# Encoder trunk on one core: mLSTM value products in full fp32 from unsplit weights, and another order of fills and first head

## The chip, the cores and the metric

The kernel runs on one core of one Trainium2 chip. The metric is the device time of one execution in microseconds; the time before is the median of three runs. The profile comes from one execution of its own, whose time stands beside its span below. PE is TensorE, DVE VectorE, ACT ScalarE, POOL GpSimd; SP's queue issues most loads.

## The reference

A trunk of two layers on 512 positions of width 1024 (batch 1, fp32). Layer 0 mixes by pooling and attention, layer 1 by a bidirectional matrix memory (mLSTM), and each layer ends with a SwiGLU mixer. The change is in layer 1's mixer, which is, in short:

```python
def mlstm_mixer(h, w_in, conv_w, conv_b, gate_b, head_gain, w_out):
    z = h @ w_in                                    # q,k | v | o | gates
    qk = silu(centred_depthwise_conv(qk_raw, conv_w, conv_b))
    ...
    h_fwd = mlstm_chunkwise(q, k, v, g[0, 0], log_sigmoid(g[0, 1]))
    h_bwd = flip(mlstm_chunkwise(flip(q), flip(k), flip(v), ...))
    hs = rms_norm((h_fwd + h_bwd)...) * head_gain
    return (sigmoid(o) * hs).reshape(B, S, -1) @ w_out
# per head and direction, with b = cumsum(log f):
#   D[t, s] = b[t] - b[s] + i[s]  (s <= t),   m[t] = max over s
#   s[t, s] = (q[t] . k[s]) * exp(D[t, s] - m[t])
#   h[t]    = sum_s s[t, s] v[s] / max(|sum_s s[t, s]|, exp(-m[t]))
```

There are 8 heads; a head has 64 query and key columns and 128 value columns. The chunked scan of the reference computes the same as this sum over all s.

## The kernel before

**Number forms.** Products of activations and weights are made of three fp32r matmuls, high x high, high x low and low x high part (`mm3`, through `mm` at line 79). A slab of weights is 256 columns of a matrix: two loads of 512 KB on SP's queue, and for each an ACT cast to the high part (`whi`) and a DVE subtraction to the low part (`wlo`), in `split` (lines 117 and 121). At most three slabs are loaded or in use; `free_slabs` starts the next.

**Layer 1's mixer** is `odd`. It begins with a gate stage (some 580 to 640 us): the projection of pair 0's queries and keys and of its values together with the gates; then `gate_chain`, a generator that computes the running sums and maxima of the gates in steps, and beside it, one step of the chain for each step of these, the projections `project_qk` and `project_v` of pair 1. Pair p holds heads 2p and 2p+1. `take_qk` takes a projection through the 5-tap convolution and the SiLU: per half (queries, keys) an ACT copy into `pad`, ACT and four DVE taps into `cy` (lines 1050 to 1054), tanh, a product, and conversions into fp32r high and low parts (`unit`, lines 1063 to 1071). `pad` and `cy` have one buffer each, in a pool `gc` of the gate stage.

Then `memory` computes the heads, in 10 slots. The pool `pw` that holds its tiles is opened when the pools of the gate stage are closed, in their place; a tile waits for the ones that were there. Slot h holds `weights(h)`: for each direction three matmuls that put the exponents into two banks (`pbd`, `pbm`) and seven exponentials (lines 1177 and 1181) that write `w`, 1280 columns: the 10 of 16 blocks of 128 x 128 that the direction needs; four `scores(h, sb)`: two matmuls and three or four DVE products that multiply `w` (lines 1194 and 1199); `halves(h)`: `w` is split into an fp32r high part `ph` (ACT, line 117) and low part `pl` (DVE, line 121). The value products of a head, `values(h, tb)`, are made in the next slot, and `finish(h)`, which normalises a head, gates it and turns it into the output projection's input, in the slot after that. In the last slots the output projection `project` begins.

Between these, `fill(n)` takes n steps of a generator of work that no head waits for at once, of 32 steps per piece: three products of 256 columns to a step, or, for queries and keys, three of 512 columns to two steps. The pieces of before: output gate 0, pair 2's queries and keys, output gate 1, values 2, queries and keys 3, output gate 2, values 3, output gate 3. `FILL = (16, 2, 2)`: 16 steps behind `weights`, 2 behind each `values`, 2 behind each `scores`.

**Banks.** Of the eight, three go around among `pbd`, `pbm`, `psS` (scores), the gates' banks and `phT`, five among all the rest: projections, value products (`ppv`), output projection.

**Order.** A scheduler sorts each engine's instructions: what was written first goes first if a simulated time line has it ready, and later work may go ahead of what is not. Engines then run their instructions in that order. `behind(ins)` forbids that an engine's instructions written inside it go ahead of `ins` on that engine.

Of the kernel before, what the change touches and what calls it, by code (L numbers as in the profile page):

```python
# [15 lines left out]
P = 128  # L16
# [18 lines left out]
WINDOW_STEPS = (1, 3, 8, 13)  # L35
POOL_STEP = 12
FILL = (16, 2, 2)
LOW_HALVES = "vv"
GATE_STEPS = (10, 10)


# [14 lines left out]
class Trunk:  # L56
# [835 lines left out]
    def odd(self, x):  # L892
        nc, a, tc = self.nc, self.a, self.tc
        with ExitStack() as es:
# [13 lines left out]
            with ExitStack() as es2:  # L908
                gp = self.open(es2, "gp", 1, side="right")
                zg = gp.tile([P, NTB, 32], F32, name="zg")  # L910
                tri = gp.tile([P, 2, P], F32, name="tri")
                nc.scalar.dma_start(tri, a["k_mask"].rearrange("d p t -> p d t"))
                nc.gpsimd.tensor_copy(self.tri, tri)
                s0 = self.next_slab()
                gw = self.gate_weights(gp)
                self.want(*[(a["w_od"][i], e) for i, e in (
                    (qk[1], "v"), (vs[1], "v"), (og[0], "v"), (qk[2], "v"), (og[1], "v"), (vs[2], "v"), (qk[3], "v"),
                    (og[2], "v"), (vs[3], "v"), (og[3], "v"))])
                self.load_slabs()
                v0 = self.values_tile()  # L920
                qk0 = [self.bank(f"pqk{1 + i % 2}") for i in range(4)]
                for hf in range(2):
                    ts = slice(hf * HS, (hf + 1) * HS)
                    pv = [self.bank("pvg") for _ in range(2)]
                    gens = [self.gemm_nat(pv[j][:, 0:288], gw, x, 2 * hf + j, 0, 288) for j in range(2)]
                    g2 = [self.gemm(qk0[2 * hf + b][:, 0:HS], s0, b, x, ts) for b in range(2)]
                    if hf == 0:
                        gens, g2 = g2 + gens, []
                    for k in range(KD):
                        for gg in gens:  # L930
# [17 lines left out]
                box = []  # L948
                for _ in self.project_qk(gc, 1, x, box):
                    next(gates, None)  # L950
                st[1] = box.pop()
                for _ in self.project_v(1, x, box):
                    next(gates, None)
                vals = {0: v0, 1: box.pop()}
                drain(gates)
            pw_es = es.enter_context(ExitStack())
            pw = self.open(pw_es, "pw", 1, side="right")
# [5 lines left out]
            self.memory(pw, x, st, vals, proj)  # L963
            pw_es.close()
            self.xp = self.open(self.ctx, "xq", 1)
            self.restore()
# [38 lines left out]

    def values_tile(self):

        t = self.od.tile([P, NTB, 2, 258], F32R, name="vx", tag="vx", bufs=2)
        self.nc.vector.tensor_copy(t[:, :, :, 256:258], self.ones[:, 0:16].rearrange("p (a b c) -> p a b c", a=4, b=2))
        return t  # L1010

    def take_values(self, vx, tb, ps):
        pv = ps.rearrange("p (h d) -> p h d", h=2)
        self.split(vx[:, tb, :, 0:128], vx[:, tb, :, 128:256], pv)

    def project_v(self, p, x, box):
        vx = self.values_tile()
# [5 lines left out]
        self.free_slabs()  # L1023
        box.append(vx)

    def project_qk(self, pool, p, x, box):
        slab = self.next_slab()
        pss = []
        for b in range(2):
            ps = self.bank("pqk")  # L1030
            for _ in self.gemm(ps, slab, b, x, slice(0, S)):
                yield
                yield
            pss.append([ps])
        self.free_slabs()
        box.append(self.take_qk(pool, p, pss))

    def take_qk(self, pool, p, pss):

# [96 lines left out]
        self.free_slabs()  # L1136
        box.append(og)

    def memory(self, pw, x, st, vals, tail):

        nc = self.nc
        off = ({0: 512, 1: 896, 2: 1152}, {3: 512, 2: 896, 1: 1152})
        span = tuple({sb: ((sb + 1, NTB) if d == 0 else (0, sb)) for sb in off[d]} for d in range(2))
        og, wt, parts, sums = {}, {}, {}, {}

        def due():
            box = []
            for kind, p in (("o", 0), ("q", 2), ("o", 1), ("v", 2), ("q", 3), ("o", 2), ("v", 3), ("o", 3)):
                if kind == "o":
                    yield from self.project_o(p, x, box)  # L1150
                    og[p] = box.pop()
                elif kind == "q":
                    yield from self.project_qk(pw, p, x, box)
                    st[p] = box.pop()
                else:
                    yield from self.project_v(p, x, box)
                    vals[p] = box.pop()

        rest = due()

        def fill(n, g=rest):
            for _ in range(n):
                next(g, None)

        def weights(h):
            for d in range(2):
                w = pw.tile([P, 1280], F32, name="w", tag="w", bufs=2)
                r = d * 32 + h
                row = self.idp[:, r:r + 1].broadcast_to([P, P])
                bd, bc = self.bank("pbd"), self.bank("pbm")  # L1170
                nc.tensor.matmul(bd, lhsT=row, rhs=self.nm, start=True, stop=False)
                nc.tensor.matmul(bd.rearrange("p (b t) -> p b t", t=P), lhsT=self.idp,
                                 rhs=self.tri[:, d:d + 1, :].broadcast_to([P, NTB, P]), start=False, stop=True)
                nc.tensor.matmul(bc, lhsT=row, rhs=self.nm, start=True, stop=True)
                for sb in range(NTB):
                    c = slice(sb * P, (sb + 1) * P)
                    nc.scalar.activation(w[:, c], bd[:, c], AF.Exp, bias=self.u_nat[:, d, sb, h:h + 1], scale=1.0)
# [7 lines left out]
        def scores(h, sb):  # L1185
# [2 lines left out]
            ps = self.bank("psS")  # L1188
            c = slice(sb * P, (sb + 1) * P)
            nc.tensor.matmul(ps, lhsT=kd[:, c], rhs=qd, start=True, stop=False)  # L1190
            nc.tensor.matmul(ps, lhsT=kd[:, c], rhs=ql, start=False, stop=True)
            for d in range(2):
                w = wt[h, d]
                nc.vector.scalar_tensor_tensor(w[:, c], ps[:, c], 0.03125, w[:, c], op0=ALU.mult, op1=ALU.mult)
# [4 lines left out]
                    nc.vector.scalar_tensor_tensor(w[:, o:o + n], ps[:, t0 * P:t1 * P], 0.03125, w[:, o:o + n],  # L1199
                                                   op0=ALU.mult, op1=ALU.mult)  # L1200

        def halves(h):
            for d in range(2):
                ph = pw.tile([P, 1280], F32R, name="ph", tag="ph", bufs=2)
                pl = pw.tile([P, 1280], F32R, name="pl", tag="pl", bufs=2)
                self.split(ph, pl, wt.pop((h, d)), lo_eng=LOW_HALVES[d])
                parts[h, d] = (ph, pl)

        def where(d, sb, tb):
            if sb == tb:  # L1210
                return slice(sb * P, (sb + 1) * P)
# [2 lines left out]

        def values(h, tb, between):
            vx = vals[h // 2]
            po = []
            for d in range(2):
                ps = self.bank("ppv")[:, 0:258]
                sbs = range(tb + 1) if d == 0 else range(tb, NTB)  # L1220
                seq = [(sb, i) for sb in sbs for i in range(2)]
                for n, (sb, i) in enumerate(seq):
                    nc.tensor.matmul(ps, lhsT=parts[h, d][i][:, where(d, sb, tb)], rhs=vx[:, sb, h % 2], start=(n == 0),  # L1223
                                     stop=(n == len(seq) - 1))
                po.append(ps)
            if tb == 0:
                sums[h] = pw.tile([P, NTB, P], F32, name="hs", tag="hs", bufs=2)
            both = self.sm.tile([P, HS], F32, name="hb", tag="hm")
            nd = pw.tile([P, 2], F32, name="nd", tag="nd", bufs=4)
            for d in range(2):  # L1230
                nc.scalar.activation(nd[:, d:d + 1], po[d][:, 256:257], AF.Abs)
            next(between, None)
            nc.vector.tensor_tensor(nd, nd, self.floor[:, :, tb, h], op=ALU.max)
            nc.vector.reciprocal(nd, nd)
            next(between, None)
            nc.scalar.activation(both, po[0][:, 0:256], AF.Identity, scale=nd[:, 0:1])
            nc.vector.scalar_tensor_tensor(both, po[1][:, 0:256], nd[:, 1:2], both, op0=ALU.mult, op1=ALU.add)
            next(between, None)
            nc.vector.tensor_tensor(sums[h][:, tb], both[:, 0:128], both[:, 128:256], op=ALU.add)
            next(between, None)  # L1240

        def finish(h):
# [22 lines left out]
        for slot in range(10):  # L1265
            old = finish(slot - 2) if slot >= 2 else iter(())
            if slot < 8:
                weights(slot)
            if slot < 8:
                fill(FILL[0])  # L1270
            else:
                drain(rest)
                fill(16 if slot == 8 else 4, tail)
# [9 lines left out]
                    scores(slot, sb)  # L1283
                    fill(FILL[2])
            drain(old)
            if slot < 8:
                halves(slot)


def constants():  # L1290
# [101 lines left out]
```

## Time and profile before

| | |
|---|---|
| median of three runs | 1237.44 us (1235.94 to 1244.37) |
| profiled execution | 1235.73 us, span 1233.9 us |
| PE | 1208.7 us busy, 98% |
| DVE | 682.2 us, 55% |
| ACT | 500.8 us, 41% |
| POOL | 136.6 us, 11% |
| granted PE clock, mean | 0.994 |

Busy times are shares of the span. Matmuls are pipelined and drawn longer than the time from one to the next, so the PE's share is no measure of its pace. In the rows, L79 is the helper through which all projections go; their banks tell them apart: `pqk` queries and keys, `pv` values, `po` output gates, `pout` output projection. A full fp32 matmul stands as two rows of the PE, an fp32r one as one; the rows' types say f32 for both.

### The profile page before, as it was taken

How to read it: one execution, taken by the hardware profiler on the slowest of the kernel's cores; microseconds unless marked ns; L12 is line 12 of the kernel's file. 1: busy time of each engine (PE TensorE's matmuls, PEld its weight loads, DVE VectorE, ACT ScalarE, POOL GpSimd, SP SyncE). 2: the span in 40 equal slices, each digit the busy share in tenths (PEclk: the TensorE clock that was granted, in tenths of full speed). 3: DMA queues.
4: the chain of work that ended last, by engine and by line, in shares of the span. 5: the costliest groups of instructions: out<-in, count | busy, mean ns of one | idle time of the engine just before them, and what ended most of it. 6: DMA issues, size and time to landing. Idle time of an engine off the chain costs nothing.

```text
span 1233.9 us, 17427 instructions
## 1 busy us (share of the span) xinstructions
PE 1208.7 (98%) x6930; PEld 1030.8 (84%) x6930; DVE 682.2 (55%) x1174; ACT 500.8 (41%) x950; POOL 136.6 (11%) x151
## 2 busy tenths in 40 slices
PE   8999999999999999999998998999999999999998
PEld 6675789988888888889896987989988888888888
DVE  4575866465755476336787887766632323233223
ACT  4466764432122221224567776743532223221321
POOL 0033220111001100110000101110011001100110
PEclk9999999999999999999999998999999999999999
DMA  9515612256745375233431211232242323233232
GB/s 389 222 57 206 234 35 93 95 223 237 275 160 215 137 278 199 76 96 127 148 103 35 68 36 35 69 99 87 90 137 86 120 69 119 86 103 103 70 101 78
DMA packets 43170, 160.19 MB, mean 130 GB/s; under 512 B 4560, under 2 KB 11344, under 8 KB 36944
## 3 DMA queue, kind: packets, MB, share of 16 engines
q1 hardware_dynamic: 42240, 158.75, 37.0%
q8 instruction: 54, 0.88, 0.3%
q10 hardware_dynamic: 848, 0.33, 0.1%
q14 instruction: 28, 0.23, 0.1%
HBM read 154.87 MB, written 4.19 MB: 129 GB/s over the span
## 4 chain that ended last, share of the span: by engine, by line
PE 91%; DVE 4%; ACT 2%; DMA 1%; issue 1%; POOL 0%; SPq 0%; DVEq 0%; ACTq 0%; POOLq 0%
PE pf L79 53%; PE pout L79 12%; PE po L79 3%; PE pv L79 3%; PE z L79 3%; PE ppv L1223 3%; PE pqk L79 2%; PE pu L79 2%; PE pav L875 2%; PE pada L79 1%; PE ppt L863 1%; DVE wlo L121 1%; PE psc L841 1%; PE pvg L79 1%; PE psc L842 1%
## 5 line engine op out<-in xcount | busy, mean ns | idle before, releaser
L79 PE MATMUL pf<-p_lo,whi 128*128 128x512 f32 (+1 forms) x1024 | 383.0, 376 | 0.0
L79 PE MATMUL pf<-p_hi,wlo 128*128 128x512 f32 (+1 forms) x1024 | 382.7, 376 | 0.0
L79 PE MATMUL pf<-p_hi,whi 128*128 128x512 f32 (+1 forms) x1024 | 380.4, 377 | 1.2 <-ACT p_hi L366 1.2
L117 ACT CAST whi<-wraw 128x1024 fp32r<-128x1024 f32 (+1 forms) x193 | 190.8, 1025 | 333.0 <-PE pf L79 238.2
L121 DVE TENSOR_TENSOR wlo<-wraw,whi 128x1024 fp32r<-128x1024 f32 (+1 forms) x193 | 230.3, 1223 | 127.8 <-ACT whi L117 125.5
L79 PEld LDWEIGHTS pf<-p_hi,wlo 128*128 128x128 f32 x1024 | 192.5, 188 | 35.1
L79 PEld LDWEIGHTS pf<-p_lo,whi 128*128 128x128 f32 x1024 | 192.7, 188 | 34.8
L79 PEld LDWEIGHTS pf<-p_hi,whi 128*128 128x128 f32 x1024 | 190.9, 188 | 35.8 <-ACT p_hi L366 1.4
L121 POOL TENSOR_TENSOR p_lo<-gf,p_hi 128x512 fp32r<-128x512 f32 (+1 forms) x48 | 70.5, 1472 | 582.5 <-ACT p_hi L117 582.5
L675 DVE TENSOR_TENSOR gf<-pf,si 128x512 f32<-128x512 f32 (+1 forms) x48 | 31.1, 647 | 164.3 <-PE pf L79 149.4
L79 PE MATMUL pout<-p_hi,whi 128*128 128x256 f32 x320 | 91.5, 287 | 0.3 <-DVE xT L333 0.3
L79 PE MATMUL pout<-p_lo,whi 128*128 128x256 f32 x320 | 90.7, 284 | 0.0
L79 PE MATMUL pout<-p_hi,wlo 128*128 128x256 f32 x320 | 90.0, 283 | 0.0
L117 ACT CAST p_hi<-gf 128x512 fp32r<-128x512 f32 (+1 forms) x48 | 27.9, 582 | 114.7 <-DVE gf L675 114.7
L246 DVE SCALAR_TENSOR_TENSOR aacc<-araw,silc,aacc 128x1024 f32<-128x1024 f32 x49 | 65.4, 1335 | 13.2 <-DMA araw<-in_ada_r_dram 11.8
L79 PEld LDWEIGHTS pout<-p_hi,whi 128*128 128x128 f32 x320 | 61.1, 191 | 3.0 <-issue 1.5
L79 PEld LDWEIGHTS pout<-p_lo,whi 128*128 128x128 f32 x320 | 61.2, 191 | 0.4
L79 PEld LDWEIGHTS pout<-p_hi,wlo 128*128 128x128 f32 x320 | 60.9, 191 | 0.4
L718 DVE SCALAR_TENSOR_TENSOR xT<-pf,mod,xT 128x512 f32<-128x512 f32 x32 | 24.0, 749 | 67.1 <-PE pf L79 66.9
L673 ACT ACTIVATE si<-pf 128x512 f32<-128x512 f32 (+1 forms) x48 | 26.7, 557 | 75.7 <-PE pf L79 75.6
L79 PE MATMUL pout<-unit,whi 128*128 128x256 f32 x256 | 47.6, 285 | 0.8 <-ACT unit L1261 0.8
L333 DVE SCALAR_TENSOR_TENSOR xT<-pout,mod,xT 128x256 f32<-128x256 f32 x64 | 28.9, 479 | 30.7 <-PE pout L79 30.5
(253 smaller groups left out, 1875.2 us busy)
## 6 DMA issues: line engine op xcount, KB each, us to landing
wraw<-in_w_dram SPq DMA_DIRECT2D x130, 512.0 KB, 4.6
araw<-in_ada_r_dram SPq DMA_DIRECT2D x40, 1024.0 KB, 6.4
wraw<-in_w_od_dram SPq DMA_DIRECT2D x24, 512.0 KB, 4.6
araw<-in_ada_a_dram SPq DMA_DIRECT2D x8, 1024.0 KB, 15.7
wraw<-in_w_eo_dram SPq DMA_DIRECT2D x10, 512.0 KB, 4.7
wraw<-in_w_oo_dram SPq DMA_DIRECT2D x10, 512.0 KB, 3.7
wraw<-in_w_qkv_dram SPq DMA_DIRECT2D x6, 512.0 KB, 15.2
wraw<-in_w_dram SPq DMA_DIRECT2D x10, 256.0 KB, 2.7
```

What stands on the lines that cost most here:

```text
L79: self.pe_last = self.nc.tensor.matmul(*args, **k)
L117: nc.scalar.copy(hi, src)
L121: eng.tensor_tensor(lo, src, hi.bitcast(F32), op=ALU.subtract)
L246: nc.vector.scalar_tensor_tensor(acc, src, s, acc, op0=ALU.mult, op1=ALU.add)
L333: nc.vector.scalar_tensor_tensor(xs, ps, self.mcol(layer, vec, m), xs, op0=ALU.mult, op1=ALU.add)
L673: nc.scalar.activation(si[:, :n], p1, AF.Silu)
L675: ins = nc.vector.tensor_tensor(gf[:, :n], p3, si[:, :n], op=ALU.mult)
L718: nc.vector.scalar_tensor_tensor(self.xT[:, m], ps, self.mcol(layer, 5, m), self.xT[:, m], op0=ALU.mult, op1=ALU.add)
L841: nc.tensor.matmul(ps, lhsT=self.qst[:, h, qs], rhs=self.kst[:, 2 * kv], start=True, stop=False)
L842: self.sc_ins = nc.tensor.matmul(ps, lhsT=self.qst[:, h, qs], rhs=self.kst[:, 2 * kv + 1], start=False, stop=True)
L875: nc.tensor.matmul(po[c, 0:HS], lhsT=self.vst[:, k, c], rhs=pt_of[pr, j][:, k], start=(k == 0), stop=(k == 3), tile_position=(0, 64 * j))
L1223: nc.tensor.matmul(ps, lhsT=parts[h, d][i][:, where(d, sb, tb)], rhs=vx[:, sb, h % 2], start=(n == 0), stop=(n == len(seq) - 1))
```

## The change

Five things change:

1. The value products use `w` itself, in fp32, and values in fp32: `halves` goes, the values' low part goes, and a value tile has 130 columns for a head (128 values and two ones) in place of 258. The two directions' sums go into one bank, and the division and sum of the two directions take 128 columns in place of 256, with one addition less.
2. `w` gets four buffers in place of two.
3. The fills become one list, `due`, that begins with values 1 and queries and keys 1; 62 of its steps are taken beside the gate chain and the rest in `memory`. So pair 1's values come ahead of its queries and keys (their slabs too), and the last step of the latter and their `take_qk` fall into slot 0, with `pad` and `cy` in `pw`.
4. A `fill` in `memory` is put behind the second last matmul of the list `core` (the last exponent matmul of each direction, and the second matmul of each score).
5. In slot 0 the scores come right behind the weights, with two steps behind each, and the other 24 steps behind them.

```diff
+                vals, self.og = {0: v0}, {}
+                rest = self.due(x, st, vals)
+                for _ in range(62):
+                    next(rest)
                     next(gates, None)
-                st[1] = box.pop()
-                for _ in self.project_v(1, x, box):
-                    next(gates, None)
-                vals = {0: v0, 1: box.pop()}
                 drain(gates)
...
-        t = self.od.tile([P, NTB, 2, 258], F32R, name="vx", tag="vx", bufs=2)
-        self.nc.vector.tensor_copy(t[:, :, :, 256:258], self.ones[:, 0:16].rearrange("p (a b c) -> p a b c", a=4, b=2))
+        t = self.od.tile([P, NTB, 2, 130], F32, name="vx", tag="vx", bufs=2)
+        self.nc.vector.memset(t[:, :, :, 128:130], 1.0)
...
-        pv = ps.rearrange("p (h d) -> p h d", h=2)
-        self.split(vx[:, tb, :, 0:128], vx[:, tb, :, 128:256], pv)
+        self.nc.scalar.copy(vx[:, tb, :, 0:128], ps.rearrange("p (h d) -> p h d", h=2))
...
-        box.append(self.take_qk(pool, p, pss))
+        box.append(self.take_qk(self.pw, p, pss))
...
+    def due(self, x, st, vals):
+
+        box = []
+        for kind, p in (("v", 1), ("q", 1), ("o", 0), ("q", 2), ("o", 1), ("v", 2), ("q", 3), ("o", 2), ("v", 3), ("o", 3)):
...
+        core = [None, None]
 
         def fill(n, g=rest):
-            for _ in range(n):
-                next(g, None)
+            with self.behind(core[-2]):
+                for _ in range(n):
+                    next(g, None)
...
-                w = pw.tile([P, 1280], F32, name="w", tag="w", bufs=2)
+                w = pw.tile([P, 1280], F32, name="w", tag="w", bufs=4)
...
-                nc.tensor.matmul(bc, lhsT=row, rhs=self.nm, start=True, stop=True)
+                core.append(nc.tensor.matmul(bc, lhsT=row, rhs=self.nm, start=True, stop=True))
...
-            nc.tensor.matmul(ps, lhsT=kd[:, c], rhs=ql, start=False, stop=True)
+            core.append(nc.tensor.matmul(ps, lhsT=kd[:, c], rhs=ql, start=False, stop=True))
...
-        def halves(h):
-            for d in range(2):
-                ph = pw.tile([P, 1280], F32R, name="ph", tag="ph", bufs=2)
-                pl = pw.tile([P, 1280], F32R, name="pl", tag="pl", bufs=2)
-                self.split(ph, pl, wt.pop((h, d)), lo_eng=LOW_HALVES[d])
-                parts[h, d] = (ph, pl)
...
-            for d in range(2):
-                ps = self.bank("ppv")[:, 0:258]
-                sbs = range(tb + 1) if d == 0 else range(tb, NTB)
-                seq = [(sb, i) for sb in sbs for i in range(2)]
-                for n, (sb, i) in enumerate(seq):
-                    nc.tensor.matmul(ps, lhsT=parts[h, d][i][:, where(d, sb, tb)], rhs=vx[:, sb, h % 2], start=(n == 0),
-                                     stop=(n == len(seq) - 1))
-                po.append(ps)
+            ps = self.bank("ppv")[:, 0:260].rearrange("p (d c) -> p d c", d=2)
+            seq = [(d, sb) for d in range(2) for sb in (range(tb + 1) if d == 0 else range(tb, NTB))]
+            for n, (d, sb) in enumerate(seq):
+                nc.tensor.matmul(ps[:, d], lhsT=wt[h, d][:, where(d, sb, tb)], rhs=vx[:, sb, h % 2], start=(n == 0),
+                                 stop=(n == len(seq) - 1))
...
-            for d in range(2):
-                nc.scalar.activation(nd[:, d:d + 1], po[d][:, 256:257], AF.Abs)
+            nc.scalar.activation(nd.rearrange("p (d c) -> p d c", d=2), ps[:, :, 128:129], AF.Abs)
...
-            nc.scalar.activation(both, po[0][:, 0:256], AF.Identity, scale=nd[:, 0:1])
-            nc.vector.scalar_tensor_tensor(both, po[1][:, 0:256], nd[:, 1:2], both, op0=ALU.mult, op1=ALU.add)
+            nc.scalar.activation(both[:, 0:P], ps[:, 0, 0:P], AF.Identity, scale=nd[:, 0:1])
+            nc.vector.scalar_tensor_tensor(sums[h][:, tb], ps[:, 1, 0:P], nd[:, 1:2], both[:, 0:P], op0=ALU.mult, op1=ALU.add)
...
-            nc.vector.tensor_tensor(sums[h][:, tb], both[:, 0:128], both[:, 128:256], op=ALU.add)
...
+            if slot == 0:
+                for sb in range(NTB):
+                    scores(0, sb)
+                    fill(FILL[2])
+                fill(FILL[0] + 4 * FILL[1])
+                continue
...
-            if slot < 8:
-                halves(slot)
```

## Rows read from the trace of the kernel before

**Rows 1.** Windows (us from the start): length, each engine's busy time (instructions), clock, DMA.

```profile
640.00:700.00 60.00, 55.11 (x352) 47.43 (x351) 49.74 (x118) 44.45 (x117) 5.76 (x9) 0.97 0.16 54
...
730.00:760.00 30.00, 24.26 (x148) 21.80 (x148) 24.43 (x57) 21.25 (x56) 2.74 (x4) 0.89 0.12 36
760.00:820.00 60.00, 60.00 (x473) 58.30 (x473) 44.98 (x124) 38.55 (x113) 7.27 (x12) 1.00 0.17 54
820.00:840.00 20.00, 18.21 (x137) 16.49 (x136) 11.93 (x32) 8.36 (x26) 1.21 (x2) 1.00 0.41 132
```

**Rows 2.** Groups by form, PE, 640 to 840 us: busy us, mean ns, idle before.

```profile
L1223 PE MATMUL ppv<-vx,ph 128*128 128x258 f32 x160 | 41.3, 291 | 2.9 <-ACT pad L1050 0.8 <-ACT ph L117 0.8 <-ACT hb L1236 0.7
...
L79 PE MATMUL po<-whi,p_hi 128*128 128x256 f32 x125 | 36.7, 294 | 4.2 <-ACT hb L1236 2.0 <-DVE hb L1237 1.7 <-ACT og L1134 0.5
...
L79 PE MATMUL pout<-unit,whi 128*128 128x256 f32 x123 | 23.3, 288 | 0.8 <-ACT unit L1261 0.8
L79 PE MATMUL pv<-wlo,p_hi 128*128 128x256 f32 x64 | 18.1, 282 | 0.0
...
L1190 PE MATMUL psS<-unit 128*128 128x512 f32 x32 | 13.8, 430 | 1.4 <-ACT w L1181 0.6 <-DVE w L1194 0.5 <-ACT w L1177 0.3
...
L79 PE MATMUL pqk<-p_lo,whi 128*128 128x512 f32 x32 | 12.6, 393 | 0.0
...
L1174 PE MATMUL pbm<-nm,ident 128*128 128x512 f32 x15 | 6.4, 423 | 2.5 <-ACT w L1177 2.5
```

**Rows 3.** Chain that ended last, dense runs: start us, us, what and how many.

```profile
63.21 0.79 PE prs L79 x8
...
721.34 4.79 PE pqk L79 x21
...
765.42 1.43 PE po L79 x12
...
799.09 1.20 PE ppv L1223 x10
...
852.18 0.44 PE pbc L79 x4
```

**Rows 4.** The same chain at the first head.

```profile
638.82 0.23 PE pbd L1172
639.06 11.52 PE po L79 x96
...
655.60 0.62 ACT unit L1070
...
656.24 1.14 ACT w L1177 x4
657.38 1.10 ACT w L1181 x3
```

**Rows 5.** Waits of the PE, 735 to 752 us: total us, times, longest.

```profile
PE po L79 <- ACT hb L1236: 2.0, 1, 2.0
PE po L79 <- DVE hb L1237: 1.7, 1, 1.7
PE pbm L1174 <- ACT w L1177: 1.1, 1, 1.1
```

**Rows 6.** The same chain behind that stretch, and at the last head.

```profile
750.93 5.49 PE po L79 x24
...
831.70 0.70 ACT unit L1261
...
832.42 0.76 DVE unit L1262
```

**Rows 7.** Groups by form, DVE and then ACT, 600 to 840 us.

```profile
L1054 DVE SCALAR_TENSOR_TENSOR cy<-pad,cols,cy 128x512 f32<-128x512 f32 x32 | 24.0, 751 | 2.9 <-ACT cy L1051 2.5
L121 DVE TENSOR_TENSOR pl<-w,ph 128x1280 fp32r<-128x1280 f32 x16 | 23.6, 1485 | 0.3 <-ACT ph L117 0.3
...
L117 ACT CAST ph<-w 128x1280 fp32r<-128x1280 f32 x16 | 19.8, 1263 | 2.6 <-DVE w L1194 2.5
```

More of the change, by code (lines that the diff above doesn't have):

```diff
@@ L37 @@
 FILL = (16, 2, 2)
-LOW_HALVES = "vv"
 GATE_STEPS = (10, 10)
@@ L916, in odd @@
                 self.want(*[(a["w_od"][i], e) for i, e in (
-                    (qk[1], "v"), (vs[1], "v"), (og[0], "v"), (qk[2], "v"), (og[1], "v"), (vs[2], "v"), (qk[3], "v"),
+                    (vs[1], "v"), (qk[1], "v"), (og[0], "v"), (qk[2], "v"), (og[1], "v"), (vs[2], "v"), (qk[3], "v"),
                     (og[2], "v"), (vs[3], "v"), (og[3], "v"))])
@@ L947, in odd @@
                 next(gates)
-                box = []
-                for _ in self.project_qk(gc, 1, x, box):
+                vals, self.og = {0: v0}, {}
+                rest = self.due(x, st, vals)
+                for _ in range(62):
+                    next(rest)
                     next(gates, None)
-                st[1] = box.pop()
-                for _ in self.project_v(1, x, box):
-                    next(gates, None)
-                vals = {0: v0, 1: box.pop()}
                 drain(gates)
             pw_es = es.enter_context(ExitStack())
-            pw = self.open(pw_es, "pw", 1, side="right")
+            self.pw = self.open(pw_es, "pw", 1, side="right")
             self.mix = ([None] * KD, [None] * KD)
@@ L962, in odd @@
             proj = self.project(0, slabs, range(4), self.mix, KD, 1, 2, acc[0])
-            self.memory(pw, x, st, vals, proj)
+            self.memory(st, vals, rest, proj)
             pw_es.close()
@@ L1024, in project_v, with project_qk @@
         box.append(vx)
-    def project_qk(self, pool, p, x, box):
+    def project_qk(self, p, x, box):
         slab = self.next_slab()
@@ L1137, in project_o, with memory @@
         box.append(og)
-    def memory(self, pw, x, st, vals, tail):
-        nc = self.nc
+    def due(self, x, st, vals):
+        box = []
+        for kind, p in (("v", 1), ("q", 1), ("o", 0), ("q", 2), ("o", 1), ("v", 2), ("q", 3), ("o", 2), ("v", 3), ("o", 3)):
+            if kind == "o":
+                yield from self.project_o(p, x, box)
+                self.og[p] = box.pop()
+            elif kind == "q":
+                yield from self.project_qk(p, x, box)
+                st[p] = box.pop()
+            else:
+                yield from self.project_v(p, x, box)
+                vals[p] = box.pop()
+    def memory(self, st, vals, rest, tail):
+        nc, pw, og = self.nc, self.pw, self.og
         off = ({0: 512, 1: 896, 2: 1152}, {3: 512, 2: 896, 1: 1152})
         span = tuple({sb: ((sb + 1, NTB) if d == 0 else (0, sb)) for sb in off[d]} for d in range(2))
[L1144 to L1159, printed above, removed]
+        wt, sums = {}, {}
+        core = [None, None]
         def fill(n, g=rest):
-            for _ in range(n):
-                next(g, None)
+            with self.behind(core[-2]):
+                for _ in range(n):
+                    next(g, None)
         def weights(h):
             for d in range(2):
-                w = pw.tile([P, 1280], F32, name="w", tag="w", bufs=2)
+                w = pw.tile([P, 1280], F32, name="w", tag="w", bufs=4)
                 r = d * 32 + h
@@ L1216, in values @@
             vx = vals[h // 2]
-            po = []
-            for d in range(2):
-                ps = self.bank("ppv")[:, 0:258]
-                sbs = range(tb + 1) if d == 0 else range(tb, NTB)
-                seq = [(sb, i) for sb in sbs for i in range(2)]
-                for n, (sb, i) in enumerate(seq):
-                    nc.tensor.matmul(ps, lhsT=parts[h, d][i][:, where(d, sb, tb)], rhs=vx[:, sb, h % 2], start=(n == 0),
-                                     stop=(n == len(seq) - 1))
-                po.append(ps)
+            ps = self.bank("ppv")[:, 0:260].rearrange("p (d c) -> p d c", d=2)
[3 more added lines that the diff above has]
+                                 stop=(n == len(seq) - 1))
             if tb == 0:
```

## Prediction

> **What bounds the kernel now.** The windows view comes first, to find where TensorE (PE) is not the limit [rows 1]. Between 760 and 820 us it is busy for all 60 us at full granted clock; in 640 to 700 us 4.9 us are idle and the granted clock falls to 0.97 of full speed on the mean, in 730 to 760 us 5.7 and 0.89, and after 820 us 1.8 are idle. All three lie in the mLSTM's memory stage, 640 to 840 us. A busy PE is not a PE at its pace (a matmul that stands alone is drawn 0.3 to 0.5 us long), so I count instead. The forms of the PE in that stage [rows 2]: 320 value products (two rows of 160), 377 for the output gate (three rows), 192 for later values (three), 181 of the output projection (two), 64 scores (two), 96 of the query and key projection (three), 43 for the weights' exponents (three), and 32 transposes of 128 columns, near the 0.110 us of the 128-wide products. What one costs in a dense run is read from the chain that ended last [rows 3]: 4.79/21 = 0.228 us at 512 columns, 1.43/12 = 0.119 at 256, 1.20/10 = 0.120 at 258. So the stage needs 750 x 0.119 + 320 x 0.120 + 203 x 0.228 + 32 x 0.11 = 177.4 of its 200 us: **22.6 us are lost**, and the rest of the PE's work is bound by its own pace. The same count by window: 640 to 700 us (265 narrow, 83 wide, 4 transposes) loses 9.1; 730 to 760 (113, 31, 4) loses 9.0; 820 to 840 (133 narrow, 4) loses 3.8; 0.7 is left elsewhere. What the change is worth is what it gets back of these, plus what it saves at the PE's pace.
>
> **Part A, the products.** Out: 320 products of 258 fp32r columns at 0.120. In: 160 products of 130 columns in full fp32. The trace of before has fp32 products elsewhere, and each leaves two records: two 128-column products (L79, pbc) are four records in 0.44 us, 0.110 each; and 128 fp32 weight columns against two moving ones (prs) take 0.79/8 = 0.099, so the load is not longer than that [rows 3]. I take 0.111, by the row nearest in width: 320 x (0.120 - 0.111) = **2.9 us saved**. Bounds: 0 if the records keep the old products' 0.120, 3.2 at 0.110.
>
> The rows above show an fp32 weight load of at most 0.099 us. The Trainium skill (TensorE: Matmul & The Clock Gate, section Weight-path perf modes) says that fast weight load is on only for inputs that are not fp32, and measured it at about twice the speed. By it the new products could lose what the old ones perhaps had; nothing in the sum uses this, and it stands below as a rival with a price from rows.
>
> **Part B, the first head.** In the chain [rows 4] the first five of the six matmuls for head 0's exponents end with the one at 638.82 us, then 96 products of output gate 0 run to 650.6. The first exponential (L1177) comes at 656.24, some 17 us after its bank was written, right behind the last conversions of the second query-key pair (L1070): `w` stands in the pool that opens where the gate pools were, and that pair's `pad` and `cy` are still in use there. By then the scheduler has issued the fills of slot 0 and half of slot 1, and the PE waits for bank after bank. The change removes that cause: pair 1's convolution goes to the new pool and into slot 0's fills. What is moved with it: per pair 8 taps on VectorE at 0.75 us [rows 7] and 8 more VectorE instructions, no longer than a tap apart from four tiny memsets: at most 12 us of VectorE; twelve ScalarE instructions, at most 10 us. They now run beside output gate 0 and q2 (32 steps of 3 x 0.119 and 16 products x 3 x 0.228 = 22 us of PE work), and head 2, the first that reads them, has its scores at the end of slot 2; nobody waits. The end of pair 1's projection also frees a slab, and with it go two loads on SP's queue and the casts and subtractions of that slab; they come some 3 us later than the same loads now (two steps and the first head's matmuls lie before them), for products two slots away: nothing. POOL has only the gates' additions behind it. The swap of v1 and q1 costs nothing on the PE: same products, same slabs, and the gate steps come every 3 x 0.119 instead of every 1.5 x 0.228.
> What is late next: head 0's own chain. One direction's exponentials are 1.14 + 1.10 us [rows 4]; the three banks shared with the scores let the second direction's last matmul start only after four of them, and the fills are now queued behind the second last core matmul, so two to four of these waits, 0.3 to 1 us each, stay open. I leave **2.5 us** of the 9.1: 6.6 gained. Bounds: nothing left, 9 gained; or 6 left, 3 gained, if ScalarE is busy with a slab's casts at that time.
>
> **Part C, 730 to 760 us.** The waits there [rows 5]: 2.0 and 1.7 us for banks that L1236 and L1237 had yet to read, 1.1 for an exponential that could not write because `w` (two buffers) was still being read by the splits. Then, behind the longest of these idle times, the PE comes back at the lower of its two clock levels (1.2 GHz of 2.4): 24 products take 5.49 us, 0.229 each against 0.119, 2.6 us [rows 6]. The change takes out the splits, 23.6 us of VectorE and 19.8 of ScalarE in 16 pairs [rows 7], gives `w` four buffers, and halves the banks of the value products (one for both directions, 32 in place of 64 in the stage) and the columns of L1236 and L1237. What stays is pair 3's convolution in the same place, and the slab splits. I leave **1.5 us** of 9.0: 7.5 gained; the clock loss goes with the idle time before it. Bounds: 9 and 4 (waits halved, clock loss still there in part).
>
> **Part D, the tail.** Of the 3.8 us, 1.8 are idle [rows 1] and the rest is matmuls that stand alone; the waits for banks among the last head's products go with the halved banks. The last head's ScalarE and VectorE steps, 0.70 and 0.76 us [rows 6], have no fill left and stay: 2.0 of 3.8 remain, **1.8 gained** (bounds 0 and 2.4).
>
> **Part E, the tie.** Each `fill` is now queued on the PE behind the second last core matmul. Behind such a matmul wait up to 16 steps, 16 x 3 x 0.119 = 5.7 us of work, and behind those the value products. In slots where nothing is lost now (700 to 730, 760 to 820) it can only cost. No row shows a tied order; the nearest is the one wait of L1174 in the disturbed stretch, 1.1 us [rows 5], against none where nothing is lost. VectorE and ScalarE, which read those banks, are relieved of the splits. I take 0.6 us lost in all, near to the stretches without loss; bounds 0 and 5, which is 0.6 in each of eight slots.
>
> **Sum.** 2.9 + 6.6 + 7.5 + 1.8 - 0.6 = 18.2 us. The profiled execution took 1235.7 us, so 1217.5; it lies 1.7 under the median of the three runs, so 1219 against 1237.4. All bounds at their good ends (3.2, 9, 9, 2.4, 0) give 23.6 and 1214; at their bad ends 0 + 3 + 4 + 0 - 5 = 2, 1235.
>
> **Rivals.**
> 1. *The convolutions, not the splits, hold the engines.* The taps, the slab splits and the exponentials stay as they are. If the banks still come late around pair 3's convolution, C gains 2 and B half: 2.9 + 3.3 + 2 + 1.8 - 0.6 = 9.4, 1228. For it: the two longest waits end at L1236 and L1237 [rows 5], short instructions that stood in queues among such steps; the taps alone are 24.0 us in 32 [rows 7]. Against: the taps of that one pair are 6 us of it, and more than that in splits leaves the same queues.
> 2. *The first head does not come early.* If `w` waits for the rest of the gate pools (pair 0's convolution shares `pad` and `cy`, one buffer), B's 6.6 stay lost: 1226. For it: the four convolutions run one after the other now. Against: the exponentials follow pair 1's last conversion within 0.03 us [rows 4], so all that is older was free before it, though the rows don't say since when.
> 3. *The tie makes the PE wait: slower.* Place: the head of every slot, where the first direction's third matmul needs a bank that the previous head's scores still hold, with 16 steps queued behind it, which now can't go ahead. Price: if both directions' exponentials are paid in the open less the two steps let in between, 4.5 - 0.7 = 3.8 us in 8 slots is 30 us, against 18 gained and the 0.6 already counted: 1249. It makes the kernel slower from 2.3 us per slot on. For it: the scheduler's reordering is what keeps 760 to 820 us full now. Against: only what is behind the second last core matmul is bound, and that one was emitted a step before.
> 4. *fp32 weights load slowly* (the rule cited above: its sentence stands in part A). Twice the old pace, 0.24 a record, is 320 x 0.12 = 38 us against the 15.3 of the other parts: 1260. Against it the rows with fp32 weights, 0.099 and 0.110.
>
> **How the numbers follow.** My forecast has 0.68, rival 1 0.12, rival 2 0.09, rival 3 0.08, rival 4 0.03. A change of 1% (12.4 us, to 1225.1) is about what a measurement of this kernel can tell from none. Nearly all of the forecast's own range (1212 to 1226) is under it: faster 0.69; rivals 1 and 2 and the mild part of 3 are within it: 0.25; slower 0.06. The range of 8 in 10 takes in rivals 1 and 2 and most bounds: 1211 to 1233.
>
> **What would show it.** Right: the first L1177 by 641 us instead of 656; no wait of the second direction's L1174 above 1 us; granted clock 1.00 in all windows of the stage; value products as 320 records at 0.11 us; stage shorter by about 18 us with the same fills; no idle above 1 us between 640 and 820. Wrong: idle PE in front of L1174 or L1190 at every slot's head (rival 3), L1177 of head 0 still late (2), waits for L1237 or L1050 around pair 3 (1), value records near 0.2 us (4).

## The result, and the profile after

| | before | after |
|---|---|---|
| median | 1239.09 us (1235.94 to 1244.37, 4 runs) | 1217.52 us (1217.32 to 1219.41, 4 runs) |
| ratio after / before | | 0.9824, 95% interval 0.9802 to 0.9846 |
| profiled execution | 1235.73 us, span 1233.9 | 1219.41 us, span 1217.6 |

The change makes the kernel 1.8% faster; 1219 us was predicted. Timed again on another chip it stood at 1221.91 us against 1238.33, 0.9867 (0.9852 to 0.9882): the two intervals don't meet, so 0.4% is not settled by one set of runs here, and small differences are taken below from kernels of one batch, or from the count in the stage.

Line numbers have moved: `mm` is L78, the value product L1210, the exponent matmuls L1168, L1169 and L1171, the exponentials L1174 and L1178, the scores L1187 and L1188. First the windows of the kernel after, with the columns of [rows 1].

```profile
640.00:700.00 60.00, 58.99 (x401) 53.61 (x400) 49.04 (x124) 46.67 (x124) 6.99 (x12) 1.00 0.27 92
...
730.00:760.00 30.00, 30.00 (x219) 28.25 (x219) 25.49 (x68) 22.93 (x64) 4.80 (x8) 1.00 0.12 38
760.00:820.00 60.00, 59.30 (x479) 57.46 (x479) 30.52 (x92) 27.32 (x85) 5.24 (x10) 1.00 0.15 53
820.00:840.00 20.00, 20.00 (x172) 20.00 (x171) 9.29 (x20) 6.78 (x13) 0.70 (x1) 1.00 0.18 60
```

Against [rows 1] the idle time in 640 to 700 us falls from 4.9 to 1.0 us, in 730 to 760 from 5.7 to none, and the granted clock is 1.00 in each. VectorE (DVE) and ScalarE (ACT) are hardly less busy in the first two windows (49.04 and 25.49 us of DVE; 49.74 and 24.43 before): more work passes in the same time. Their relief shows from 760 us on, 30.5 us of DVE instead of 45.0, and in the whole execution:

```profile
PE 1201.2 (99%) x6930; PEld 1027.5 (84%) x6930; DVE 646.7 (53%) x1110; ACT 476.2 (39%) x902; POOL 136.0 (11%) x151
```

The same number of PE instructions is there: 320 records of value products as before, in another form. The forms of the PE answering to [rows 2] (620 to 860 us, so that the whole stage is in):

```profile
L78 PE MATMUL pout<-unit,whi 128*128 128x256 f32 x256 | 47.4, 286 | 0.7 <-ACT unit L1245 0.7
L1210 PE MATMUL ppv<-vx,w 128*128 128x130 f32 x320 | 40.9, 275 | 0.0
L78 PE MATMUL po<-whi,p_hi 128*128 128x256 f32 x128 | 37.1, 290 | 0.0
...
L1187 PE MATMUL psS<-unit 128*128 128x512 f32 x32 | 12.8, 400 | 0.2 <-DVE unit L1246 0.2
...
L1171 PE MATMUL pbm<-nm,ident 128*128 128x512 f32 x16 | 6.5, 406 | 0.8 <-ACT w L1174 0.5 <-DVE w L1196 0.3
```

What is to be seen is the last column: the idle time in front of the output gates and the value products is gone. The waits of the PE from 636 to 860 us, answering to [rows 5], are all that is left (the lines left out belong to the FFN behind the stage):

```profile
PE pout L78 <- ACT unit L1245: 0.7, 1, 0.7
...
PE pbm L1171 <- ACT w L1174: 0.5, 1, 0.5
PE pbm L1171 <- DVE w L1196: 0.3, 1, 0.3
PE psS L1187 <- DVE unit L1246: 0.2, 1, 0.2
```

Then the chain that ended last, at the first head, answering to [rows 4]:

```profile
640.16 0.23 PE pbd L1168
640.40 0.24 PE pbd L1169
...
640.66 1.15 ACT w L1174 x4
...
641.85 0.50 PE pbm L1171
...
643.05 0.40 PE psS L1187
...
648.27 7.54 PE po L78 x63
```

The first exponential starts 0.02 us behind its bank, at 640.66 us; before it came almost 18 us behind (some 17 behind the bank of the other direction, from which the prediction counts). The same view at the last head, answering to [rows 3, 6]:

```profile
803.08 1.11 PE ppv L1210 x10
...
806.03 6.51 PE pout L78 x55
...
813.49 0.70 ACT unit L1245
...
814.21 0.76 DVE unit L1246
...
815.02 13.81 PE pout L78 x109
```

A value record now takes 1.11/10 = 0.111 us (0.112 in others of these dense runs), and the last head's conversions still stand alone between 813.47 and 815.02 us with nothing beside them, though most of the 109 products that follow need only the heads before.

**The count.** As in the prediction: elapsed time of the stage less each matmul at its dense pace (0.112 us for the new records); what is left over is called lost. The stage, from the first exponent matmul to the last product of the output projection, fell from 227.6 to 207.2 us, and the loss in it from 22.6 to 4.1 us. The loss and the faster records make 18.5 + 2.6 = 21 us; three products of pair 1's queries and keys, 0.7 us, have moved into the stage. The profiled spans differ by 16.3 us and not by 21, because the parts around the stage, which the edits change little or not at all, lost 5.9, 4.7 and 3.7 us in the profiled execution of before (up to layer 1's mixer, in its first projections, in the FFN behind it) and 7.2, 6.3 and 5.6 in that of after. Among the profiled executions of all kernels here these three range from 5.9 to 11.5, 4.7 to 9.1 and 3.7 to 7.7 us.

### The profile page after: what moved, and what is told of

It reads as the page before. It is cut to its first block, busy times and chain, and to the rows that moved or that the text cites. A ratio compares the mean times of both kernels' runs of the same rounds, so it can differ in the third digit from the quotient of the medians.

```text
span 1217.6 us, 17268 instructions
## 1 busy us (share of the span) xinstructions
PE 1201.2 (99%) x6930; PEld 1027.5 (84%) x6930; DVE 646.7 (53%) x1110; ACT 476.2 (39%) x902; POOL 136.0 (11%) x151
## 4 chain that ended last, share of the span: by engine, by line
PE 93%; DVE 3%; DMA 2%; issue 1%; ACT 1%; POOL 0%; ACTq 0%; DVEq 0%; POOLq 0%
PE pf L78 53%; PE pout L78 11%; PE po L78 4%; PE pqk L78 3%; PE ppv L1210 3%; PE pv L78 3%; PE z L78 3%; PE pu L78 2%; PE pav L874 2%; PE pada L78 1%; PE ppt L862 1%; DVE wlo L120 1%; PE psc L840 1%; PE pvg L78 1%; DMA wraw<-in_w_od_dram 1%
## 5 line engine op out<-in xcount | busy, mean ns | idle before, releaser
L78 PE MATMUL pf<-p_lo,whi 128*128 128x512 f32 (+1 forms) x1024 | 383.0, 376 | 1.0 <-DVE p_lo L366 1.0
L78 PE MATMUL pf<-p_hi,wlo 128*128 128x512 f32 (+1 forms) x1024 | 382.7, 376 | 0.0
L78 PE MATMUL pf<-p_hi,whi 128*128 128x512 f32 (+1 forms) x1024 | 380.5, 377 | 1.7 <-ACT p_hi L365 1.7
L78 PEld LDWEIGHTS pf<-p_lo,whi 128*128 128x128 f32 x1024 | 192.7, 188 | 36.0 <-DVE p_lo L366 1.2
L78 PEld LDWEIGHTS pf<-p_hi,wlo 128*128 128x128 f32 x1024 | 192.5, 188 | 34.8
L78 PEld LDWEIGHTS pf<-p_hi,whi 128*128 128x128 f32 x1024 | 190.9, 188 | 36.6 <-ACT p_hi L365 2.1
L78 PE MATMUL pout<-p_hi,whi 128*128 128x256 f32 x320 | 91.5, 287 | 0.3 <-DVE xT L332 0.3
L78 PE MATMUL pout<-p_lo,whi 128*128 128x256 f32 x320 | 90.7, 284 | 0.0
L78 PE MATMUL pout<-p_hi,wlo 128*128 128x256 f32 x320 | 90.0, 283 | 0.0
L78 PEld LDWEIGHTS pout<-p_hi,whi 128*128 128x128 f32 x320 | 61.1, 191 | 3.0 <-issue 1.5
L78 PEld LDWEIGHTS pout<-p_lo,whi 128*128 128x128 f32 x320 | 61.2, 191 | 0.4
L78 PEld LDWEIGHTS pout<-p_hi,wlo 128*128 128x128 f32 x320 | 60.9, 191 | 0.4
L78 PE MATMUL pout<-unit,whi 128*128 128x256 f32 x256 | 47.4, 286 | 0.7 <-ACT unit L1245 0.7
## 6 DMA issues: line engine op xcount, KB each, us to landing
wraw<-in_w_qkv_dram SPq DMA_DIRECT2D x6, 512.0 KB, 15.5
```

Of the source, the lines that this page charges most:

```text
L78: self.pe_last = self.nc.tensor.matmul(*args, **k)
```

## The experiments

All in one table first. "Lost" is the count above, for one profiled execution of each kernel: up to the first value product, from there to the last product of output gate 3, and behind that. Batch 1 is fp32only to twobanks, batch 2 after_again to pair1, batch 3 the rest; each has its own runs of before on its chip.

| kernel | median us | ratio to before (95%) | lost: first head | middle | end | sum |
|---|---|---|---|---|---|---|
| before | 1237.8 to 1239.1 | 1 | 5.7 | 13.0 | 3.8 | 22.6 |
| after | 1217.52 | 0.9824 (0.9802 to 0.9846) | 1.0 | 1.4 | 1.7 | 4.1 |
| fp32only: items 1 and 2 alone | 1225.91 | 0.9883 (0.9851 to 0.9915) | 4.0 | 3.8 | 1.7 | 9.5 |
| order: items 3 to 5 alone | 1232.18 | 0.9951 (0.9934 to 0.9967) | 1.3 | 11.6 | 2.6 | 15.5 |
| notie: after without item 4 | 1215.63 | 0.9816 (0.9786 to 0.9846) | 0.1 | 0.5 | 1.7 | 2.2 |
| twobanks: after, a bank for each direction | 1224.30 | 0.9884 (0.9857 to 0.9911) | 1.0 | 7.7 | 2.5 | 11.2 |
| after_again | 1221.91 | 0.9867 (0.9852 to 0.9882) | 1.0 | 1.4 | 1.7 | 4.1 |
| notie_tail: no tie, last fills kept | 1215.81 | 0.9819 (0.9797 to 0.9841) | 0.1 | 0.5 | 0.3 | 0.9 |
| notie_slot0: items 4, 5 undone | 1216.56 | 0.9817 (0.9799 to 0.9835) | 0.1 | 0.5 | 1.7 | 2.3 |
| pair1: item 3 undone | 1238.47 | 1.0007 (0.9992 to 1.0022) | 19.9 | 1.8 | 1.7 | 23.4 |
| notie_twobanks | 1219.11 | 0.9857 (0.9835 to 0.9878) | 0.1 | 2.0 | 2.4 | 4.5 |
| notie_pair1 | 1224.92 | 0.9897 (0.9877 to 0.9916) | 4.4 | 3.9 | 1.7 | 10.0 |
| notie_order: items 3 and 5 alone | 1237.52 | 0.9997 (0.9984 to 1.0009) | 0.1 | 18.2 | 2.6 | 20.8 |

The theory behind them: two causes, each with its own place. The splits and the second bank hold ACT and DVE so long that banks come late (730 to 760 us and the tail), and the gate pool holds up head 0. The first rival: the convolutions hold the engines and the splits don't matter.

**fp32only.** The kernel before with unsplit fp32 products in one bank and four buffers of `w`; its order is left as it was.

```diff
-                w = pw.tile([P, 1280], F32, name="w", tag="w", bufs=2)
+                w = pw.tile([P, 1280], F32, name="w", tag="w", bufs=4)
...
             drain(old)
-            if slot < 8:
-                halves(slot)
```

(`values`, `values_tile` and `take_values` are those of the change.)

> The kernel before with items 1 and 2 alone: unsplit fp32 value products in one bank, and four buffers of w; order, fills and pair 1 as before. My theory: the products give 320 x (0.120 - 0.112) = 2.6 us, and without the splits and with half the banks the 9.0 us lost at 730 to 760 us and 2.0 of the 3.8 at the tail come back, while the first head keeps its 9.1: 1239 - 13.6 = about 1225. Rival, the new order does it and the splits were covered: 2.6 us alone, about 1236.

Measured: 1225.91 us, and the loss in 730 to 760 us is gone without any change of order. Of the 9.5 us that are left, 7.5 are lost before 700 us (the first value product falls in this stretch, so the table has part of it in the middle), and they begin at the first head, in the chain that ended last:

```profile
644.78 11.52 PE po L79 x96
...
662.04 0.69 DVE unit L1070
...
662.77 1.14 ACT w L1176 x4
```

The last conversion of pair 1, 0.04 us of memsets of `pad`, and only then the first exponential, at 662.77 for a bank that was written before 645: [rows 4] again. The rival (the splits don't matter) had the time of before, and falls.

**order.** The change with items 1 and 2 undone: split products, two banks, `w` in two buffers.

```diff
                 fill(FILL[0] + 4 * FILL[1])
+                halves(0)
                 continue
...
             drain(old)
+            if slot < 8:
+                halves(slot)
```

> The kernel after with items 1 and 2 undone: split products in two banks and two buffers of w, with pair 1 behind the gates, the tie and the new slot 0. My theory: the first head's loss of 9.1 us falls to about 2, 7 us gained, and the loss around pair 3's convolution stays or moves: 1232, between 1229 and 1236. Rival, the new order does it: 1221 or less.

Measured: 1232.18 us, as expected. The first head comes early and loses 1.3 us, but a loss of 6.5 us opens at 670 to 690 us, where pair 2's convolution runs beside head 1's splits; the kernel before, with the same two side by side there, lost 2.1. The longest wait of the PE, then the chain behind it:

```profile
PE po L78 <- ACT hb L1234: 4.7, 1, 4.7
```

```profile
675.58 1.05 ACT whi L116
...
676.69 0.52 ACT pad L1054
...
677.50 1.15 ACT ph L116
...
679.94 0.50 ACT unit L1060
...
680.47 0.63 ACT unit L1061
...
681.11 0.48 ACT hb L1234
...
681.64 4.62 PE po L78 x24
```

The short `hb` stands on ACT behind a slab's cast, the split of `w` and two conversions; 24 products then take 4.62 us, 0.193 each against 0.119 (granted clock 0.64 in that stretch). So the first rival has a point: convolution and splits together hold the engines. Either one alone passes: before loses 0.2 us at 700 to 730 us, where heads are split and no convolution's taps run, and fp32only 0.1 at 730 to 760 us, where pair 3's convolution runs and no head is split.

**notie.** The change without item 4.

```diff
-            with self.behind(core[-2]):
-                for _ in range(n):
-                    next(g, None)
+            for _ in range(n):
+                next(g, None)
```

> The kernel after with item 4 undone: fills may go ahead of any core matmul. My theory: the tie neither costs nor brings 2 us, 1216 to 1220, since the exponentials and scores now keep up. Rival, the tie is what holds fills back for the heads: at least 8 of the 22 us are lost again, 1226 or more. A second rival, the tie costs: 1215 or less.

Measured: 1215.63 us, between the theory's range and the second rival's; the medians don't part them, the count does. Of the stage's 4.1 lost 1.9 go, all of them ahead of 700 us, where the PE is now busy without a gap:

```profile
640.00:700.00 60.00, 60.00 (x416) 55.61 (x415) 50.83 (x127) 47.81 (x127) 8.32 (x12) 1.00 0.33 103
```

There are 416 matmuls in the window against 401. So the second rival is right as to the sign, and the tie cost about three times the 0.6 us of part E.

**twobanks.** The change with the value products' two directions in a bank each, so 64 banks in the stage instead of 32, and one more tiny ACT instruction for each.

```diff
-            ps = self.bank("ppv")[:, 0:260].rearrange("p (d c) -> p d c", d=2)
+            ps = [self.bank("ppv")[:, 0:130] for _ in range(2)]
...
```

> The kernel after with a bank of its own for each direction's value products (64 banks in place of 32 in the stage, two small ScalarE instructions for one). My theory: banks ran short only where the engines that read them were late, and without the splits they are not: 1 to 2 us slower, 1218.5 to 1219.5. Rival, the shared bank is what cleared 730 to 760 us and the tail: 5 to 10 us slower, 1223 or more.

Measured: 1224.30 us. That is 6.8 above after's first set of runs and 2.4 above its second, whose interval overlaps with this one's; the count is clearer, the middle loses 7.7 us instead of 1.4. The theory, in which the second bank was a side matter, doesn't fit that. The rival has the size; its reason, that the value products run short of banks, explains the least of it. The three longest waits, then the chain behind the second:

```profile
PE pbm L1171 <- ACT w L1174: 1.9, 2, 1.4
PE pbd L1168 <- DVE w L1196: 1.8, 1, 1.8
PE ppv L1211 <- ACT hb L1223: 0.9, 1, 0.9
```

```profile
746.51 1.52 POOL hr L126
...
748.32 1.02 DVE hs L1239 x3
...
750.99 0.47 DVE w L1196
...
755.99 0.34 DVE w L1196
...
756.47 0.47 PE pbd L1168
```

DVE reaches the gating of a finished head (`hs` L1239) before POOL has its root (`hr`), waits 0.9 us, and the score products (`w` L1196) queue behind, among other work; the PE's next exponent matmul needs their bank. The banks of the two longest waits are thus not the doubled ones, only that of the third is. And the wait for `hr` goes with the second bank: DVE stands for it at all 8 heads here (13.3 us in sum) and in notie_twobanks (9.8), at 4 to 6 heads in the three kernels with two banks and splits, at 1 or 2 in all with one bank (after: once, 1.8). Why a second bank puts the gating ahead of its root is not traced further.

**after_again, notie_tail, notie_slot0, pair1** ran as one batch, to set the parts side by side on one chip.

> The kernel after itself, to compare the next three with on the same chip: 1217 to 1219, a ratio of 0.982 to 0.984 to the kernel before.

Measured: 1221.91 us, 3 to 5 us above what was expected. The profiled stage loses what it did in the first set, to 0.1 us; as far as the two profiled executions show, the sets differ outside it (9.9 us lost up to layer 1's mixer instead of 7.2).

**notie_tail.** Without the tie, and with the output projection's steps kept for the last head's conversions:

```diff
-                fill(16 if slot == 8 else 4, tail)
+                if slot == 9:
+                    drain(old)
+                fill(4 if slot == 8 else 16, tail)
```

> The kernel after without item 4, and with the last steps of the output projection's first half kept for the end: 4 in place of 16 before the last head's products and 16 in place of 4 behind its last steps, which are written ahead of them. Theory: the tie costs the 2.0 us by which the stage of the run without it lost less (2.2 against 4.2 us), and the tail's 1.8 us go because products are left to run beside the last head's two conversions: 3.8 us faster than the kernel after, 1214. Rival: the tail is only moved, since the norm that follows waits for the same last product: 1216.

Measured: 1215.81 us, 6.1 below after_again. The gap at the last head has closed, in the chain that ended last:

```profile
812.00 0.11 PE phT L1241
812.11 17.19 PE pout L78 x141
```

141 products in a row at 0.122 where after had 109 behind a gap of 1.5 us. The stage's loss is 0.9 us; against notie_slot0 in the same batch the medians don't tell the gain of some 1.4 us from none.

**notie_slot0.** Without the tie, and slot 0 like any other slot (its `if slot == 0` block taken out).

> The kernel after without items 4 and 5: no tie, and slot 0 as the other slots, its scores behind 24 steps. Theory: head 0's exponentials come early because of item 3, and the values of head 0 are far enough behind either way: same as without the tie alone, 1215 to 1217. Rival, item 5 matters: the first head loses 2 us or more, 1218 or more.

Measured: 1216.56 us and the losses of notie. Item 5 is worth nothing that shows once the tie is out. Against after_again in the same batch the two kernels without the tie are 5 to 6 us faster on the median (runs of 1213.6 to 1216.7 and 1212.9 to 1218.6 against 1220.4 to 1222.8), of which the stage's count explains 1.8 (notie_slot0) and 3.2. Where the rest lies is open: one profiled execution of each can't tell it from the swings around the stage.

**pair1.** The tie and all else kept, but pair 1's values, queries and keys back in the gate stage with its `pad` and `cy` (the list of `due` begins at output gate 0):

```diff
-                for _ in range(62):
-                    next(rest)
+                box = []
+                self.pw = gc
+                for _ in self.project_v(1, x, box):
                     next(gates, None)
+                vals[1] = box.pop()
+                for _ in self.project_qk(1, x, box):
+                    next(gates, None)
+                st[1] = box.pop()
...
```

> The kernel after with item 3 undone in the main: pair 1's values and then its queries and keys are finished beside the gates, with pad and cy in the gates' pool, and the fills begin with output gate 0. My theory: w waits for those buffers again, the first exponential comes some 15 us later than in the kernel after, and since the fills are tied behind the core the PE stands still for it: 7 to 15 us slower, 1224 to 1232. Rival, that wait had other causes: 1219 or less.

Measured: 1238.47 us, the whole gain gone and worse than either theory had it. Window, wait and chain:

```profile
640.00:700.00 60.00, 42.15 (x256) 37.40 (x255) 34.59 (x79) 34.70 (x86) 3.96 (x7) 0.86 0.25 82
```

```profile
PE pbm L1176 <- ACT w L1179: 17.6, 1, 17.6
```

```profile
657.61 0.69 DVE unit L1072
658.31 0.05 DVE pad L1047
658.39 1.21 ACT w L1179 x4
659.64 0.79 PE pbm L1176
660.43 1.28 PE po L78 x6
661.71 0.43 PE psS L1192
```

The exponentials wait for pair 1's last conversion as in the kernel before; but there 96 products of output gate 0 ran meanwhile [rows 4], and here the tie holds them behind the second last core matmul, which waits. Behind that the PE comes back at the lower of its two clock levels (granted clock 0.50 up to 663.8 us): six products in 1.28 us, 0.213 each, against 0.71 for six in after. This is rival 3 of the prediction, in one slot: with item 3 undone the tie turns a loss of 7.8 us against notie into one of 19.3 against after.

**notie_twobanks, notie_pair1, notie_order** take the tie out of three of these, to tell its share from the other's.

> Two banks for a head's two directions, and no tie. In the run with two banks and the tie the PE stood for banks of exponents and scores, behind VectorE, which in its turn stood for GpSimd's root of a head's norm. Theory A, the tie turned late engines into PE waits: without it fills go ahead, and the loss of the stage falls from 11.2 to under 5 us, 1215 to 1219. Theory B, value products run out of banks: still 9 us or more lost in the stage, 1222 to 1225.

Measured: 1219.11 us, theory A. Without the tie the second bank costs 2.3 us in the stage (4.5 against 2.2), with it 7.1 (11.2 against 4.1). The tie makes late banks dear: what would have filled the wait may not go ahead.

> Pair 1 finished beside the gates, with pad and cy in their pool, and no tie: item 3 and item 4 undone, the rest of the change in. My theory: the first exponential is as late as in the kernel before, but fills cover part of it, and the PE loses what it lost at the first head in the run with items 1 and 2 alone, 8 us, not 20: 1222 to 1227. Rival, the wait is as dear without the tie: 1234 or more.

Measured: 1224.92 us, the theory. Pair 1's convolution in the gate pool costs 7.8 us in the stage without the tie (10.0 against 2.2) and 19.3 with it (23.4 against 4.1).

> The new order with split products in two banks and two buffers of w (items 1 and 2 undone), and no tie. Theory: of the 15.5 us that the stage lost with the tie, the first head's 1.3 go, the losses around the convolutions stay near the kernel before's 9, and the time is 1226 to 1232. Rival, the tie made them: 1222 or less.

Measured: 1237.52 us, slower than expected: the new order with split products and no tie gains nothing on before, though its first head loses only 0.1 us. The middle loses 18.2 us, with waits of up to 4.7 us for exponentials in front of `pbm`. With split products the tie is thus worth 5.3 us in the stage (20.8 - 15.5), and with unsplit ones it costs some. A likely reason, not shown: with ACT and DVE this full, fills that run ahead delay the matmuls that these engines need next.

## Why the prediction was right

The two causes that it named were the right ones: items 1 and 2 take the loss from 22.6 to 9.5 us, items 3 to 5 to 15.5, both to 4.1. They don't simply add up: with split products and no tie the new order gains nothing on the median (notie_order), which the prediction, with one sum for all, could not show. Term by term:

- **Part A** took 2.9 us. A new record measures 0.111 to 0.112, so 320 x (0.120 - 0.112) = 2.6. The rule of the Trainium skill weighed there (TensorE: Matmul & The Clock Gate, section Weight-path perf modes) would have had the loads of fp32 weights slower; the records show no cost of it at 130 columns. Rival 4 falls with that.
- **Part B** left 2.5 of 9.1 us; up to 700 us the count finds 2.1. The cause is shown by pair1 and notie_pair1: item 3 is what frees `w`. But the rest is only in part where part B put it: head 0's own chain, with the fills queued behind it, is 1.0 us, and 1.1 are lost at 690 to 700 us, at a later head. notie loses 0.3 us up to 700 us, so nearly all of it is the tie. Rival 2 falls with the first exponential at 640.66 us.
- **Part C** left 1.5 of 9.0 us; nothing is left. fp32only shows that items 1 and 2 do it alone. Rival 1 is wrong for this kernel; in order, where the splits are back, convolution and splits stand together in front of the 4.7 us of `hb`. What part C didn't price by itself is the bank: by the count, one for both directions carries 7.1 us of the gain beside the tie, 2.3 without. The splits and the two buffers of `w` were not parted by any run.
- **Part D** left 2.0 of 3.8 us, and 1.7 is left: the last head's two conversions, as named. notie_tail, with 0.3 lost there, shows that it was no floor: the fills had been used up just ahead.
- **Part E** took 0.6 us, and this is the term that was mis-sized: 1.9 in the stage, and its share of the medians may be more. Its place was also off: not the slots without loss but the stretch up to 700 us. B and E together, 3.1 us by the prediction, come to 2.4 because part B had some of the tie's waits in it.

Sum by the count: 18.5 + 2.6 = 21 us against 18.2. The gain on the medians was 21.6 us in the first set of runs and 16.4 in the second, and the parts around the stage, which the prediction took as unchanged, took some 5 us back in the profiled execution. So 18.2 lies between, and a hit as near as 1219 against 1217.5 is partly chance.

Of the signs named: the first exponential by 641 us, the waits of the second direction's L1171 under 1 us, the clock, the 320 records at 0.11 us and no idle time above 1 us all came as written; the stage is 20.4 us shorter where some 18 were named.

## What to carry to other kernels

Count a stage as elapsed time less each instruction at its dense pace, and look for what frees the buffer in front of the first late instruction: here a pool's lifetime (8 us) and the splits with what hung on them, a second bank and only two buffers of `w` (13 us together), were the causes, not the engines' average load. An order that holds fill work behind a critical instruction is free only while that instruction never waits: the same tie cost 1.9 us, 6.7 with a second bank (11.2 - 4.5), 13.4 with a late pool (23.4 - 10.0), and gained 5.3 where the engines were overfull. So look at the waits of the instruction that it would hang on first: the longest in front of `pbm` were 0.5, 1.4 and 17.6 us in the three kernels where it cost. Try the parts in pairs, since what one part is worth here depends on which others are in.

## What the runs showed of the hardware

- A full fp32 product of 130 columns leaves two records of 0.112 us, 0.224 in all; it stands in the place of two fp32r products of 258 columns at 0.120 each [rows 3]. So the fp32 form is the cheaper one here on the PE too, beside the splits that it saves.
- After 17.6 us of waiting (pair1) matmuls came back at a granted clock of 0.50, 0.43 us for 512 columns against 0.23; with waits of 0.7 us and less (after) the granted clock is 1.00 in every window of the stage.
- Executions differ by several us in parts that the edits change little or not at all: 14 to 24 us were lost there in sum, and 9.9 against 7.2 up to layer 1's mixer in two executions of one kernel, after. A median of four runs can hide an edit of 2 us; the count within the stage came out the same to 0.1 us in the two executions of after, the only kernel that was profiled twice.
